# Weight sums of the output projection made in DRAM, and a rebuilt last stage, in a hybrid attention layer

## The chip, the cores and the metric

The kernel runs on one core of one Trainium2 chip. The metric is the device time of the program in microseconds (us), as the median of several runs. Before the change it is 952.56 us, the median of three runs from 950.74 to 953.96 us. One more execution was taken with the hardware profiler; all durations of single instructions come from that one.

## The reference, cut to what matters

One encoder layer in fp32 on 512 tokens of 2048 features, with 16 meta tokens put ahead of them (528 rows):

```
hn = rmsnorm(h, pre_norm_g)                       # h: (528, 2048)
qa, ka, va, ga, qb, kb, vb, gb = split(hn @ w_in)
ya = gqa_axial_mixer(qa, ka, va, ...) * silu(ga)  # mixer A: 8 heads of 128, 2 key/value heads, axial rope
yb = diff_attn_mixer(qb, kb, vb, ...) * silu(gb)  # mixer B: 8 heads, two softmaxes of 64 each, ALiBi
y  = concat([ya, yb]) @ w_out                     # (528, 2048) x (2048, 2048)
h  = h + rmsnorm(y, post_norm_g)                  # returned without the meta tokens
```

The change touches only the last two lines: the output projection, its RMSNorm and the residual sum. Mixer B is where part of the new work is put.

## The kernel before, in words

**Products and weights.** Every fp32 operand is split into a high part (rounded to fp32r) and a low part (the rest), and a product is three matmuls: high by high, low by high, high by low. `mm` (L63) issues them all. Weights come in chunks of 128x1024 (512 KB): `fetch` takes the next entry of the list `todo` two entries ahead of its use, `wload` puts the load on SP's queue (L151) into the tile `st` (three buffers), and `wsplit` makes `wh` on ACT (L158) and `wl` on DVE (L159), three buffers of each. An entry of `todo` that is a function is called in place of `wload`.

**Attention.** The program runs the input projection column by column as dense matmuls, and the attention of each head is laid between them by hand: generators in `lanes`, with delays in the table `LAG`. One head of mixer B takes about 56 us. Per head, DVE adds the ALiBi bias (L460), ACT takes the exponential (L468), DVE the reciprocal of the sum (L470), POOL multiplies by it (L473), DVE combines the two softmaxes (L475), PE transposes, ACT and DVE split the transposed result into `ph` (L313) and `pl` (L316), and PE multiplies by the values. POOL also has the small operations at L420. The output of a mixer B head is stored to DRAM as `oscr` and read back later.

**Output projection.** It has four column groups of 512. Groups 0 and 3 are made in full by `dense_out`, eight chunks each. Groups 1 and 2 are made as a 2 x 2 block product in Strassen's form as Winograd wrote it, with seven products for eight: the rows fall in two halves of 256 tokens (row tiles 0 and 1, and 2 and 3), the inner dimension in its two halves of eight heads. `block(r, c, i)` is chunk `i` of column group `1 + r` and inner half `c`; `C(r, x, u)` is that column group of row tile `2x + u`, kept in the tiles `y`. The products follow one another on PE, each with four weight chunks and 48 matmuls of 128x512; I name them by their operands in the code: y(0,0), y(1,0), t1, t2, y(1,1), t3, t4. The weights of the first two and of the last are plain blocks. Those of the others are sums: the first is block (1,0) + (1,1), for t1; block (0,0) is added for t2; block (0,1) is added for y(1,1); and the last is (0,0) + (1,0), for t3.

Before the change these sums are made in SBUF tiles `chain` (`ch` in the profile). During `dense_out(3)` POOL's queue loads block (1,0) plainly (L832) and adds (1,1) onto it by an adding transfer (L833). After each split of a chain tile, `summed` loads one further block into an `st` buffer on SP (L704) and DVE adds it (L705); for the last sum, (0,0) is loaded afresh (L701). The operands t1 to t4 are sums of half heads, loaded by `heads_of`, combined on DVE and split by `operand`; `fourth_sum`, with its two DVE additions from L842 on, runs beside t3.

**The end.** As a column group is done, ACT squares it with a sum (L855) into `ssy`, and the result is multiplied by the gain `gpB`: on DVE in `collect`, on POOL in `block_done` (L904). The row factor is made on POOL by an addition with a scale (L936) and a power of -0.5 (L938). `row_block` multiplies 512 columns by that factor and adds the residual rows on DVE (L947), or, as the variant `far`, on ACT and POOL (L944, L945), and stores them on SP. The residual rows are loaded by POOL's queue: four loads of 512 KB for tiles 0 and 1 (L955), eight of 256 KB for tiles 2 and 3 (L960), placed in the code behind t3. In t4 the first chunk is used for both row tiles, and the other three for tile 0 in full, then for tile 1; `end(u, ps)` follows each: a subtraction (L976), the square, the gain (L978), the row factor and the row blocks. A scheduler with priorities orders each engine's instructions; those called through `keep_in_program_order` keep the order of the code among themselves.

## Time and the profile before

| | |
|---|---|
| median of three runs | 952.56 us (950.74 to 953.96) |
| profiled execution, its own time | 948.18 us |
| its span | 946.3 us |
| mean granted clock of PE | 0.992 |
| PE busy | 923.7 us (98%) |
| DVE busy | 584.5 us (62%) |
| ACT busy | 487.5 us (52%) |
| POOL busy | 142.2 us (15%) |
| SP's and ACT's queue, q1 | 104.71 MB, 34.0% of 16 engines' span |
| POOL's queue, q0 | 11.54 MB, 4.1% |

PE is TensorE, DVE VectorE, ACT ScalarE, POOL GpSimd, and SP the engine that mostly issues transfers; SPq and POOLq are their queues. The chain of work that ended last, followed back from the last instruction, is 87% PE and 6% DVE. PE is busy nearly all the time; in the page's 40 slices of the span only the last shows it at 3 tenths. A row of a timeline has the start in us, the duration in us, the engine, the line, the operation, output and inputs with their shapes, and in square brackets how long the engine stood idle ahead of it and what ended that. A row of a group ends with busy time and mean ns of one. The times of the last products, by the first row of each in PE's timeline, are those in the prediction.

### The profile page before, as it was taken

What the parts mean: (1) busy time and instruction counts of PE and PEld (TensorE: products, weight loads), DVE (VectorE), ACT (ScalarE), POOL (GpSimd) and SP (SyncE); (2) the same over time, 40 slices, a digit from 0 to 9 for tenths busy, and PEclk for the clock granted to TensorE, in tenths of its full rate; (3) what the DMA queues carried; (4) which work ended last, traced back from release to release, by engine and by line L of the source; (5) the groups of instructions that cost most, each with busy time, mean ns of one, the idle gap of its engine ahead of it and who ended that gap; (6) DMA issues with size and microseconds to landing.
All of it is one profiled execution on the core that took longest, in us unless ns stands there. A gap on an engine that the chain in (4) does not pass through costs nothing.

```text
span 946.3 us, 14242 instructions
## 1 busy us (share of the span) xinstructions
PE 923.7 (98%) x5498; PEld 810.6 (86%) x5498; DVE 584.5 (62%) x1007; ACT 487.5 (52%) x845; POOL 142.2 (15%) x186
## 2 busy tenths in 40 slices
PE   9999999999999999999999999999999999999993
PEld 8899898989989899998998888888888888888872
DVE  6386575747566584866655255448554662576996
ACT  6664655637464463745643154445655743244541
POOL 0001010100001010000111041126111113300044
PEclk9999999999999999999999999999999999999996
DMA  9843222322223122222223223121222447966785
GB/s 338 257 162 99 68 88 68 101 77 92 85 68 112 67 98 79 79 84 73 79 71 97 89 77 105 65 78 57 86 71 78 131 141 204 303 219 192 222 284 205
DMA packets 40611, 117.16 MB, mean 124 GB/s; under 512 B 4672, under 2 KB 9536, under 8 KB 40416
## 3 DMA queue, kind: packets, MB, share of 16 engines
q1 hardware_dynamic: 37072, 104.71, 34.0%
q0 software_dynamic: 3328, 11.54, 4.1%
q8 instruction: 43, 0.70, 0.3%
q14 instruction: 24, 0.20, 0.1%
q10 hardware_dynamic: 144, 0.01, 0.0%
HBM read 107.85 MB, written 8.39 MB: 123 GB/s over the span
## 4 chain that ended last, share of the span: by engine, by line
PE 87%; DVE 6%; ACT 2%; POOL 2%; issue 2%; DMA 1%; DVEq 0%; POOLq 0%; ACTq 0%
PE pd L63 55%; PE po L63 16%; PE sc L63 6%; PE pv L63 5%; PE tr L66 5%; DVE wl L159 1%; DVE qn L583 1%; DVE y L947 1%; DMA st<-in_w_o_dram 1%; POOL qn L597 1%; DMA xns<-in_xn_dram 1%; PE hot L63 0%; ACT qn L655 0%; ACT jk L580 0%; PE ss L63 0%
## 5 line engine op out<-in xcount | busy, mean ns | idle before, releaser
L63 PE MATMUL pd<-xh,wh 128*128 128x264 f32 (+1 forms) x992 | 332.8, 335 | 0.0
L63 PE MATMUL pd<-xh,wl 128*128 128x264 f32 (+1 forms) x992 | 324.3, 327 | 0.3 <-DVE wl L159 0.3
L63 PE MATMUL pd<-xl,wh 128*128 128x264 f32 (+1 forms) x992 | 324.6, 327 | 0.0
L158 ACT ACTIVATE wh<-st 128x1024 fp32r<-128x1024 f32 (+2 forms) x135 | 139.9, 1039 | 190.2 <-issue 82.7
L159 DVE TENSOR_TENSOR wl<-st,wh 128x1024 fp32r<-128x1024 f32 (+2 forms) x135 | 162.2, 1202 | 108.3 <-ACT wh L158 106.7
L63 PEld LDWEIGHTS pd<-xh,wl 128*128 128x128 f32 x992 | 186.5, 188 | 17.5 <-DVE wl L159 0.7
L63 PEld LDWEIGHTS pd<-xh,wh 128*128 128x128 f32 x992 | 187.2, 189 | 12.6 <-ACT wh L158 0.2
L63 PEld LDWEIGHTS pd<-xl,wh 128*128 128x128 f32 x992 | 187.3, 189 | 11.1
L63 PE MATMUL po<-wh,oh 128*128 128x512 f32 x176 | 70.5, 401 | 0.0
L63 PE MATMUL po<-wh,ol 128*128 128x512 f32 x176 | 69.5, 395 | 0.9 <-DVE ol L316 0.9
L63 PE MATMUL po<-wl,oh 128*128 128x512 f32 x176 | 69.4, 394 | 0.0
L468 ACT ACTIVATE p<-p,mx 128x528 f32<-128x528 f32 x64 | 47.1, 736 | 43.0 <-DVE mx L460 42.7
L473 POOL TENSOR_SCALAR p<-p,sm 128x528 f32<-128x528 f32 x32 | 23.2, 725 | 268.2 <-DVE sm L470 251.5
L313 ACT ACTIVATE ph<-tr 128x512 fp32r<-128x512 f32 x64 | 37.7, 592 | 36.4 <-PE tr L66 36.1
L460 DVE CUSTOM_DVE_ANT_0 p<-sc,dist 128x528 f32<-128x528 f32 x64 | 44.9, 701 | 13.4 <-PE sc L63 13.0
L63 PE MATMUL pd<-wh,xh 128*128 128x512 f32 x128 | 52.0, 407 | 0.8 <-DVE vf L307 0.8
L316 DVE TENSOR_TENSOR pl<-tr,ph 128x512 fp32r<-128x512 f32 x64 | 43.3, 687 | 14.5 <-ACT ph L313 14.1
L66 PE MATMUL tr<-ident,p 128*128 128x128 f32 (+1 forms) x320 | 50.6, 272 | 1.4 <-DVE gA L563 1.4
L63 PE MATMUL pd<-wl,xh 128*128 128x512 f32 x128 | 50.4, 394 | 0.0
L63 PE MATMUL pd<-wh,xl 128*128 128x512 f32 x128 | 50.2, 392 | 0.0
L66 PEld LDWEIGHTS tr<-ident,p 128*128 128x128 f32 (+1 forms) x320 | 37.4, 131 | 12.6 <-DVE gA L563 1.9
L420 POOL TENSOR_SCALAR pm<-pm 32x256 fp32r<-32x256 f32 x32 | 20.0, 625 | 164.7 <-ACT pm L313 164.1
(206 smaller groups left out, 1554.3 us busy)
## 6 DMA issues: line engine op xcount, KB each, us to landing
st<-in_w_t_dram SPq DMA_DIRECT2D x82, 512.0 KB, 3.6
st<-in_w_o_dram SPq DMA_DIRECT2D x40, 512.0 KB, 4.2
st<-in_w_q_dram SPq DMA_DIRECT2D x16, 512.0 KB, 3.6
xs<-in_xT_dram SPq DMA_DIRECT2D x16, 264.0 KB, 5.2
xns<-in_xn_dram SPq DMA_DIRECT2D x8, 512.0 KB, 5.4
ch<-in_w_o_dram POOLq DMA_DIRECT2D x8, 512.0 KB, 7.9
out_dram<-y SPq DMA_DIRECT2D x16, 256.0 KB, 2.2
os<-oscr SPq DMA_DIRECT2D x6, 512.0 KB, 3.7
```

The source lines that it names most:

```text
L63: self._add(self.nc.tensor.matmul(out, lhsT, rhs, start=start, stop=stop), us)
L66: self._add(self.nc.tensor.transpose(out, in_, ident), 0.109)
L158: nc.scalar.activation(wh[:, c], st[:, c], AF.Copy)
L159: nc.vector.tensor_tensor(out=wl[:, c], in0=st[:, c], in1=wh[:, c].bitcast(F32), op=ALU.subtract)
L313: nc.scalar.activation(dst, src, AF.Copy)
L316: nc.vector.tensor_tensor(out=dst, in0=src, in1=h.bitcast(F32), op=ALU.subtract)
L420: nc.gpsimd.tensor_scalar(out=pm[32:64], in0=pm[0:32].bitcast(F32), scalar1=1.0, scalar2=1.0, op0=ALU.mult, op1=ALU.mult)
L460: nc.vector.tensor_tensor_reduce(out=two(p), in0=sc[:, :, :HALF], in1=two(dist[:, w0:w0 + NT]), scale=-0.125, scalar=3.0e38, op0=ALU.add, ...
L468: nc.scalar.activation(p2[m], p2[m], AF.Exp, scale=-1.0, bias=mx[:, m:m + 1], accum_out=sm[:, m:m + 1])
L473: nc.gpsimd.tensor_scalar(out=p2[0], in0=p2[0], scalar1=sm[:, 0:1], scalar2=1.0, op0=ALU.mult, op1=ALU.mult)
L583: nc.vector.scalar_tensor_tensor(out=raw[:, i, :], in0=raw[:, i, :], scalar=ss[:rows, i:i + 1], in1=g[:rows], op0=ALU.mult, op1=ALU.mult)
L597: nc.gpsimd.tensor_tensor(out=x, in0=x, in1=cos, op=ALU.mult)
```

## The change

It has two parts.

**Sums in DRAM.** The four sums live in 16 DRAM tiles `ws`, four for each sum (`sums[0]` to `sums[3]`, in the order above). `weigh` makes them one step at a time: it starts the adding transfer of the step before on POOL's queue (L708 of the new kernel) and the plain copy of the next step, from DRAM to DRAM, on SP's queue in program order. It is called three times in each of the heads 1 to 6 of mixer B and once in head 7, so 16 copies and 16 adds. The output projection then loads the sums as plain chunks; `chain`, its loads, its adding transfers and the twelve additions on DVE go. PE's order of matmuls stays as it is.

**The last stage.** The last product's block (1,1) is loaded into tiles `wx` while y(1,1) runs, and `apart` splits it as halves of 512 columns into slots of `oh` and `ol` that are free by then. `residual` loads one block of 128x512 of the residual rows on SP in each of the 16 steps of t1, t2, y(1,1) and t3, into other freed slots. C(0,1)'s interim sum is kept in C(1,1). POOL's gain multiplications move to DVE. The row factor becomes two small POOL operations ahead of time (`part`), a square root on ACT, whose table is loaded once early (`warm`), and a reciprocal on DVE. All row blocks are on DVE, and the end's order on DVE and ACT is fixed by `keep_in_program_order`.

The core of the diff:

```diff
-    def summed(add=None, fresh=None):
-        def step(i):
-            ws = wsplit(chain[i])
-            if fresh:
-                nc.sync.dma_start(out=chain[i], in_=block(*fresh, i))
-            if add:
-                st = wp.tile([P, 1024], F32, name="st", tag="st")
-                nc.sync.dma_start(out=st, in_=block(*add, i))
-                nc.vector.tensor_tensor(out=chain[i], in0=chain[i], in1=st, op=ALU.add)
...
+    steps = ([(sums[0][i], block(1, 0, i), block(1, 1, i)) for i in range(4)]
+             + [(sums[1][i], sums[0][i], block(0, 0, i)) for i in range(4)]
+             + [(sums[2][i], sums[1][i], block(0, 1, i)) for i in range(4)]
+             + [(sums[3][i], block(0, 0, i), block(1, 0, i)) for i in range(4)])
+    def weigh():
+        if adds:
+            dst, src = adds.pop(0)
+            nc.gpsimd.dma_start(out=dst, in_=src, accum_op=ALU.add)
+        if steps:
+            dst, src, add = steps.pop(0)
+            load(dst, src)
+            adds.append((dst, add))
+    def apart():
+        def step(i):
...
+            for j in range(2):
+                n = 8 + 2 * i + j
+                wh, wl = [op.tile([P, 512], F32R, name=f"w{x}", tag=f"o{x}{n}") for x in "hl"]
+                src = last[i][:, j * 512:(j + 1) * 512]
+                with tc.high_priority(rank[0]):
+                    hi(wh, src)
+                    lo(wl, src, wh)
...
-    todo += summed((1, 0), fresh=(0, 0)) + summed() + plain(1, 1)
+    for n in range(4):
+        todo += sums[n]
+    todo += apart()
...
+    def residual():
+        t, g = places[len(xres)]
+        n = len(xres)
+        x = op.tile([P, 512], F32, name="xr", tag=f"o{'hl'[n // 8]}{n % 8}")
+        load(x, xn[t * P:(t + 1) * P, g * 512:(g + 1) * 512])
...
-        TTp(out=C(r, x, u), in0=C(r, x, u), in1=gpB[:, g * 512:(g + 1) * 512], op=ALU.mult)
+        TTv(out=C(r, x, u), in0=C(r, x, u), in1=gpB[:, g * 512:(g + 1) * 512], op=ALU.mult)
...
+    for u, ps in enumerate(product(of_y(1, 1), pd, lambda i: load(last[i], block(1, 1, i)), late=True)):
...
-        nc.gpsimd.tensor_scalar(out=r, in0=ssy[t][:, 3:4], scalar1=sspart[t], scalar2=1.0 / DM,
-                                op0=ALU.add, op1=ALU.mult)
-        nc.gpsimd.tensor_tensor(out=r, in0=r, in1=mhalf[:, 0:1], op=ALU.pow)
+        order(nc.scalar.activation(r, r, AF.Sqrt, scale=1.0 / DM, bias=sspart[t]))
...
+    def turned(t):
+        order(nc.vector.reciprocal(out=ry[t], in_=ry[t]))
...
+    def end(u, ps):
+        last_block(u, ps)
+        by_gain(u)
+        if u == 0:
+            for g in (0, 3, 1, 2):
+                row_block(3, g)
+            turned(0)
+            for g in (0, 3):
+                row_block(0, g)
         else:
...
+            for g in (1, 2):
+                row_block(0, g)
+            turned(1)
+            for g in (0, 3, 1, 2):
+                row_block(1, g)
```

How the instructions move is shown at three places; the line numbers of added or later rows are those of the new kernel. First POOL in mixer B, in a head that has three adding transfers; `p` and `sm` are a softmax's exponentials and the reciprocal of their sum, `pm` a small operand of that head, `ws_549` to `ws_551` tiles of the second sum:

```order
-L473 TENSOR_SCALAR p<-p,sm 128x528 x3
-L420 TENSOR_SCALAR pm<-pm 32x256
+L708 DMA ws_550<-in_w_o_dram 128x1024
+L473 TENSOR_SCALAR p<-p,sm 128x528 x2
+L708 DMA ws_549<-in_w_o_dram 128x1024
 L473 TENSOR_SCALAR p<-p,sm 128x528
 L420 TENSOR_SCALAR pm<-pm 32x256
-L473 TENSOR_SCALAR p<-p,sm 128x528 x3
-L420 TENSOR_SCALAR pm<-pm 32x256
+L708 DMA ws_551<-in_w_o_dram 128x1024
```

The adding transfers stand between the softmax multiplications, which keep their own order.

Next SP around y(1,1), before. `st` and `ch` are as above:

```order
L704 DMA st<-in_w_o_dram 128x1024 x3
L701 DMA ch_8156<-in_w_o_dram 128x1024
L704 DMA st<-in_w_o_dram 128x1024
L701 DMA ch_8157<-in_w_o_dram 128x1024
L704 DMA st<-in_w_o_dram 128x1024
L701 DMA ch_8158<-in_w_o_dram 128x1024
L701 DMA ch_8159<-in_w_o_dram 128x1024
L151 DMA st<-in_w_o_dram 128x1024 x4
```

And there after the change; `xr` is a block of residual rows, `wx` a chunk of the last product's block, `ws_555` to `ws_558` are chunks of the third and fourth sum:

```order
L151 DMA st<-ws_555 128x1024
L143 DMA xr<-in_xn_dram 128x512
L143 DMA wx_8204<-in_w_o_dram 128x1024
L151 DMA st<-ws_556 128x1024
L143 DMA xr<-in_xn_dram 128x512
L143 DMA wx_8205<-in_w_o_dram 128x1024
L151 DMA st<-ws_557 128x1024
L143 DMA xr<-in_xn_dram 128x512
L143 DMA wx_8206<-in_w_o_dram 128x1024
L151 DMA st<-ws_558 128x1024
```

The loads for the sums are gone, and each step has a chunk of a sum, a block of rows and a chunk of the last product in their place.

Last DVE at the end, before. `y_8162` and `y_8163` are row tiles 0 and 1, `y_8164` and `y_8165` tiles 2 and 3; `po` is a product, `ry` a row factor, `xr` residual rows:

```order
L159 TENSOR_TENSOR wl<-st,wh 128x1024
L947 SCALAR_TENSOR_TENSOR y_8164<-y_8164,ry,xr 128x512 x3
L947 SCALAR_TENSOR_TENSOR y_8165<-y_8165,ry,xr 128x512
L976 TENSOR_TENSOR y_8162<-y_8162,po 128x512
L947 SCALAR_TENSOR_TENSOR y_8165<-y_8165,ry,xr 128x512 x2
L978 TENSOR_TENSOR y_8162<-y_8162,gpB 128x512
L947 SCALAR_TENSOR_TENSOR y_8162<-y_8162,ry,xr 128x512 x2
L976 TENSOR_TENSOR y_8163<-y_8163,po 128x512
L947 SCALAR_TENSOR_TENSOR y_8162<-y_8162,ry,xr 128x512
L947 SCALAR_TENSOR_TENSOR y_8165<-y_8165,ry,xr 128x512
L978 TENSOR_TENSOR y_8163<-y_8163,gpB 128x512
L947 SCALAR_TENSOR_TENSOR y_8163<-y_8163,ry,xr 128x512 x3
```

And after, from tile 0's subtraction on; `y_8210` to `y_8213` are row tiles 0 to 3, and the `ssy` tiles hold the row factors:

```order
L987 TENSOR_TENSOR y_8210<-y_8210,po 128x512
L993 TENSOR_TENSOR y_8210<-y_8210,gpB 128x512
L981 SCALAR_TENSOR_TENSOR y_8213<-y_8213,ssy_8217,xr 128x512 x4
L996 RECIPROCAL ssy_8214<-ssy_8214 128x1
L981 SCALAR_TENSOR_TENSOR y_8210<-y_8210,ssy_8214,xr 128x512 x2
L987 TENSOR_TENSOR y_8211<-y_8211,po 128x512
L993 TENSOR_TENSOR y_8211<-y_8211,gpB 128x512
L981 SCALAR_TENSOR_TENSOR y_8210<-y_8210,ssy_8214,xr 128x512 x2
L996 RECIPROCAL ssy_8215<-ssy_8215 128x1
L981 SCALAR_TENSOR_TENSOR y_8211<-y_8211,ssy_8215,xr 128x512 x4
```

Tile 1's subtraction now stands behind the four row blocks of tile 3 and two of tile 0, and its four row blocks are all on DVE.

More of the change, by code (lines that the diff above doesn't have):

```diff
@@ L679 @@
             todo += col(T_GA + h if h < NH else T_GB + h - NH)
-    chain = {}
+    last = {}
     def block(r, c, i):
@@ L735 @@
             v = values(pss)
+            if h:
+                weigh()
             ks = keys_B(dense_T(KEYS))
@@ L819 @@
     for i in range(4):
-        chain[i] = yp.tile([P, 1024], F32, name=f"ch{i}", tag=f"ch{i}")
+        last[i] = yp.tile([P, 1024], F32, name=f"wx{i}", tag=f"wx{i}")
     t1, t2, t3, t4 = [], [], [], []
@@ L829, in first_sums @@
         t2.append(operand("v", i, a1))
-    def first_chain(i):
-        nc.gpsimd.dma_start(out=chain[i], in_=block(1, 0, i))
-        nc.gpsimd.dma_start(out=chain[i], in_=block(1, 1, i), accum_op=ALU.add)
     def third_sum(i):
@@ L860, in collect, with product @@
         TTv(out=y[t][:, gs], in0=ps, in1=gpB[:, gs], op=ALU.mult)
-    def product(ops, pool, beside=None, done=None):
+    def product(ops, pool, beside=None, done=None, late=False):
         pss = [pool.tile([P, 512], F32, name="po", tag="pd") for _ in range(2)]
         def step(u, i, ws):
-            wh, wl = ws
             for j in range(2):
@@ L887, in product @@
         return pss
+    xres, places = {}, [(t, g) for t in (2, 3, 0, 1) for g in (0, 3, 1, 2)]
+    def residual():
[3 more added lines that the diff above has]
+        load(x, xn[t * P:(t + 1) * P, g * 512:(g + 1) * 512])
+        xres[t, g] = x
     def of_y(c, x):
@@ L920 @@
         block_done(0, 0, u)
-    for u, ps in enumerate(product(of_t(t1), pd2)):
+        part(u)
+    for u, ps in enumerate(product(of_t(t1), pd2, late=True)):
         nc.scalar.activation(C(1, 1, u), ps, AF.Copy)
-    for u, ps in enumerate(product(of_t(t2), pd2, third_sum)):
+    for u, ps in enumerate(product(of_t(t2), pd2, third_sum, late=True)):
         TTv(out=C(1, 0, u), in0=ps, in1=C(1, 0, u), op=SUB)
-        TTv(out=C(0, 1, u), in0=C(1, 0, u), in1=C(1, 1, u), op=ALU.add)
-    for u, ps in enumerate(product(of_y(1, 1), pd)):
-        TTv(out=C(0, 1, u), in0=ps, in1=C(0, 1, u), op=SUB)
+        TTv(out=C(1, 1, u), in0=C(1, 0, u), in1=C(1, 1, u), op=ALU.add)
@@ L939, in row_scale, with row_block @@
         return r
-    def row_block(t, r, x, g, far=False):
+    def row_block(t, g):
         v = y[t][:, g * 512:(g + 1) * 512]
-        if far:
-            nc.scalar.activation(v, v, AF.Copy, scale=r)
-            TTp(out=v, in0=v, in1=x, op=ALU.add)
-        else:
-            nc.vector.scalar_tensor_tensor(out=v, in0=v, scalar=r, in1=x, op0=ALU.mult,
-                                           op1=ALU.add)
-        load(out[t * P:(t + 1) * P, g * 512:(g + 1) * 512], v)
-    xl_ = [[yp.tile([P, 1024], F32, name="xr", tag=f"ch{2 * t + n}") for n in range(2)]
-           for t in range(2)]
@@ L966 @@
-    with tc.high_priority(AHEAD):
-        for t in range(2):
-            r = row_scale(2 + t)
-            for g in range(4):
-                row_block(2 + t, r, xh_[t][g], g)
-    xs = lambda t, g: xl_[t][g // 2][:, g % 2 * 512:(g % 2 + 1) * 512]
-    rs = []
-    def end(u, ps):
-        TTv(out=C(1, 0, u), in0=C(1, 0, u), in1=ps, op=SUB)
-        square(u, 2, C(1, 0, u))
-        TTv(out=C(1, 0, u), in0=C(1, 0, u), in1=gpB[:, 1024:1536], op=ALU.mult)
-        if u == 1:
-            row_block(0, rs[0], xs(0, 1), 1)
-            row_block(0, rs[0], xs(0, 2), 2)
-        rs.append(row_scale(u))
-        row_block(u, rs[u], xs(u, 0), 0, True)
-        for g in ((3,) if u == 0 else (3, 1, 2)):
-            row_block(u, rs[u], xs(u, g), g)
+        order(nc.vector.scalar_tensor_tensor(out=v, in0=v, scalar=ry[t], in1=xres[t, g],
+                                             op0=ALU.mult, op1=ALU.add))
@@ new lines, in row_block, with last_block, by_gain @@
+        load(out[t * P:(t + 1) * P, g * 512:(g + 1) * 512], v)
+    def last_block(t, ps):
+        v = y[t][:, 1024:1536]
+        order(TTv(out=v, in0=v, in1=ps, op=SUB))
+        order(square(t, 2, v))
+        ry[t] = row_scale(t)
+    def by_gain(t):
+        v = y[t][:, 1024:1536]
+        order(TTv(out=v, in0=v, in1=gpB[:, 1024:1536], op=ALU.mult))
+    def turned(t):
+        order(nc.vector.reciprocal(out=ry[t], in_=ry[t]))
+    ry = {}
+    pss = product(of_t(t3), pd, fourth_sum, late=True)
```

64 lines of the change are left out of this document (39 added, 25 removed).

## The prediction

> **What bounds the kernel now.** I read the page first, then the stretches, then PE's timeline of the last stage, the chain that ended last, and the timelines of DVE, ACT, POOL and SP at the places the change touches. The page's slices of the transfers, first to last:
> ```profile
> DMA  9843222322223122222223223121222447966785
> GB/s 338 257 162 99 68 88 68 101 77 92 85 68 112 67 98 79 79 84 73 79 71 97 89 77 105 65 78 57 86 71 78 131 141 204 303 219 192 222 284 205
> ```
> They are heavy only at both ends; 338 GB/s, with the queues nine tenths busy, is the most that any 23.7 us of this trace show. In the stretches view, the last 46 us:
> ```profile
> 900.00:946.30 46.30, 29.85 (x114) 22.56 (x112) 38.24 (x50) 13.92 (x23) 23.03 (x26) 0.84 0.70 243
> ```
> PE (second number) is busy for 29.85 of 46.30 us, at a mean granted clock of 0.84, while DVE (fourth) is busy for 38.24. PE's timeline there:
> ```profile
> 903.94 0.39 PE L63 MATMUL po<-wh,uh 128*128 128x512 f32 x1
> ...
> 915.78 0.39 PE L63 MATMUL po<-wh,vh 128*128 128x512 f32 x1
> ...
> 920.09 0.39 PE L63 MATMUL po<-wh,vl 128*128 128x512 f32 x1
> 921.59 0.50 PE L63 MATMUL po<-wl,vh 128*128 128x512 f32 x1 [1.12 <-DVE wl L159]
> ...
> 925.16 0.80 PE L63 MATMUL po<-wh,vh 128*128 128x512 f32 x1 [2.37 <-ACT wh L158]
> ...
> 933.62 0.39 PE L63 MATMUL po<-wl,vh 128*128 128x512 f32 x1
> ```
> The first row opens t3, the second t4, the last closes t4; each has 48 matmuls. Nineteen steps from 915.78 to 920.09 make 0.227 us from start to start. By that t3 would take 10.89 us and took 11.84 (0.95 lost), and t4's last matmul would start 10.66 us after its first and started 17.84 after it (7.18 lost). Of the 7.18, the five steps from 920.09 to 925.16 took 5.07 us for 1.13, so 3.94 went to the two marked gaps; the 23 steps behind took 8.46 us for 5.22, so 3.24 went to a lower clock after the second gap. What the gaps waited for stands in the chain that ended last:
> ```profile
> 908.78 3.40 DVE ts L842 x2
> ...
> 915.81 8.13 DMA st<-in_w_o_dram
> 924.05 1.07 ACT wh L158
> ```
> The last weight chunk was issued at 915.81, took 8.13 us to land among the row loads of POOL's queue, and was split only then; before it DVE stood in two ops that ran beside POOL's multiplication (3.40 for two). So this stage is bound by the work that readies weights, on DVE and in the queues, and then by the chain behind the last matmul, on DVE:
> ```profile
> 930.56 1.40 DVE L947 SCALAR_TENSOR_TENSOR y<-y,ry,xr 128x512 f32<-128x512 f32 x2
> ...
> 934.70 0.68 DVE L976 TENSOR_TENSOR y<-y,po 128x512 f32<-128x512 f32 x1
> ...
> 938.44 3.08 DVE L947 SCALAR_TENSOR_TENSOR y<-y,ry,xr 128x512 f32<-128x512 f32 x3 [0.72 <-POOL ry L938]
> ```
> PE's last result is there at 933.62 + 0.39 = 934.01; the last DVE op ends at 938.44 + 3.08 = 941.52, and 4.78 us of stores and closing follow to 946.30.
>
> **The change part by part.** *Sums.* From 850 us on, by groups, DVE does:
> ```profile
> L705 DVE TENSOR_TENSOR ch<-ch,st 128x1024 f32<-128x1024 f32 x12 | 15.1, 1261 | 0.9 <-DMA ch<-in_w_o_dram 0.9
> L947 DVE SCALAR_TENSOR_TENSOR y<-y,ry,xr 128x512 f32<-128x512 f32 x14 | 12.2, 920 | 2.3 <-POOL ry L938 2.3
> L159 DVE TENSOR_TENSOR wl<-st,wh 128x1024 fp32r<-128x1024 f32 x10 | 12.2, 1222 | 6.5 <-ACT wh L158 6.5
> ...
> L316 DVE TENSOR_TENSOR vl<-ts,vh 128x512 fp32r<-128x512 f32 x4 | 2.6, 682 | 0.0
> ```
> and POOL:
> ```profile
> L904 POOL TENSOR_TENSOR y<-y,gpB 128x512 f32<-128x512 f32 x6 | 11.0, 1834 | 51.6 <-issue 44.9 <-ACT jko L855 6.7
> ```
> The twelve adds (15.1 us) go, as do POOL's six multiplications, four of which become DVE ops of 0.68 (2.7 us) and two of which join the tail. The last product's weights are split as halves into slots of their own while y(1,1) and t3 run, so nothing is left to split in t4. Is DVE on time for t3? From y(1,1)'s start, 48 steps or 10.9 us ahead of t3's at 903.94, it has six whole splits at 1.14 from start to start (0.08 under their length, since ops overlap), eight halves and eight other 128x512 ops at 0.60, 6.8 + 4.8 + 4.8 = 16.4 us, and must be done by t3's fourth step at 903.9 + 8.2 = 912.1: 19.1 us. That fits, by 2.7. At its thinnest, the third chunk of t3, whose split stands behind two squares and two halves, I find it done 0.2 before its use. I take t3 and t4 without a wait: 0.95 and 7.18 come back, and t4 runs from 914.83 to 925.49, its result there at 925.88; PE gains 8.13.
>
> *The tail* gives some back. Its new order on DVE is fixed, and by the rows above an add or subtraction costs 0.60 behind another op (0.68 less 0.08), a row block 0.66 (1.40 for two, less 0.08). ACT's part between the subtraction and the gain:
> ```profile
> 930.73 0.63 ACT L855 ACTIVATE jko<-y 128x512 f32<-128x512 f32 x1 [5.01 <-DVE y L976]
> 931.27 0.19 ACT L855 ACTIVATION_READ_ACCUMULATOR jko<-y 128x1 f32 x1
> ```
> and from DVE's timeline in mixer B:
> ```profile
> 175.51 0.16 DVE L470 RECIPROCAL sm<-sm 128x2 f32<-128x2 f32 x1
> ```
> That is 0.73 (930.73 to 931.46) for the square, and I put 0.09 for each hand-over between the two; the DVE row is the nearest to the new reciprocal, 0.19 with its hand-over. After t3, DVE has five 0.60 ops, two reciprocals and four row blocks, 6.0 us, ending at 921.1. Tile 0's result is there after 30 matmuls of t4, at 914.83 + 29 x 0.227 + 0.39 = 921.8. From there: subtraction to 922.57, square to 923.4, gain to 924.1, four row blocks to 926.7, reciprocal 926.9, two row blocks 928.25. Only then comes tile 1's subtraction, 2.4 after PE gave its result; with the same steps it ends at 928.9, square 929.75, gain 930.45, two row blocks 931.8, reciprocal 932.0, four row blocks 934.7. That is 6.8 before 941.52. The square root (between the 0.19 and the 0.63 of the ACT rows) hides behind the gain and two row blocks, 1.9 us; were it in the open it would cost at most that 0.63. The last six stores come 0.66 apart, 262 KB each, 397 GB/s against the 338 seen: between 0 and 0.6 more at the end; I take 0.4, as 338 is a rate seen here. **Sum: -6.4 us.**
>
> *Mixer B* gets 16 copies on SP and 16 adding transfers on POOL, not in the trace. The nearest rows, of POOL, SP, DVE and PE in one head:
> ```profile
> 175.84 0.71 POOL L473 TENSOR_SCALAR p<-p,sm 128x528 f32<-128x528 f32 x1 [5.76 <-DVE sm L470]
> 180.34 0.71 POOL L473 TENSOR_SCALAR p<-p,sm 128x528 f32<-128x528 f32 x1 [3.79 <-DVE sm L470]
> ```
> ```profile
> 171.97 0.33 SPq L510 DMA_DIRECT2D oscr<-gB  x1
> ```
> ```profile
> 184.53 0.68 DVE L316 TENSOR_TENSOR pl<-tr,ph 128x512 fp32r<-128x512 f32 x1
> ```
> ```profile
> 191.41 0.28 PE L63 MATMUL pv<-pl,vh 128*128 128x256 f32 x1
> ```
> and of transfers of the same size, a plain load and the adding ones of before:
> ```profile
> st<-in_w_o_dram SPq DMA_DIRECT2D x40, 512.0 KB, 4.2
> ```
> ```profile
> L833 POOL DMA_DIRECT2D ch<-in_w_o_dram x4: 869/888/927, 793.7 to 812.5; - x4
> ...
> DMA to landing us min/median/max: 6.1/7.9/11.9
> ```
> POOL reaches an add at 176.55, behind its second softmax multiplication of a head. The copy that this add waits for stands on SP behind the store at 171.97, so it starts at about 172.3 and lands, at the 4.2 of a plain load of its 512 KB, at 176.5. The add's issue takes 0.89 and POOL is free at 177.4, 2.9 before its next op at 180.34. Behind a blocked POOL, DVE would wait, and behind DVE's wait stands the split at 184.53, read by PE at 191.41: 6.2 us of cover more. A copy of 11.9 us, the longest adding transfer, would still stay within both. So I take nothing, with 0 to +1 us, and no gain, since PE has no wait there to lose. On SP the copies stand between weight loads and wait for adds issued a head earlier. The Trainium skill, SBUF — State Buffer, section "A bandwidth-pool intuition that's wrong (but worth ruling out)", says that a POOL-issued transfer of about 620 ns alone takes about 3100 when DVE locks POOL out of the port its descriptors go through. The issues here took 869 to 927 ns, with DVE about half busy; by the page's figure the sum would not move, but the copy's cover below would shrink by 2.2 us.
>
> *Queues at the end.* POOL's twelve row loads become sixteen on SP, and the four chunks of the last product go ahead of t3's. In y(1,1) each step's rows on SP carry 524 + 262 + 524 KB. At 338 GB/s that is 3.9 us for a step of 2.8: four steps leave 4.4 us of backlog. A chunk is issued about 2.4 us after PE ends the step six before its own, and three buffers give it 8.2 - 2.4 = 5.8 us until its split can start and 3 us more until the split must; with 4.2 to land, 4.6 are to spare. Just enough, so nothing in the sum. The Trainium skill, Perfetto Trace Analysis, section "Roofline", has the 16 DMA engines at about 435 GB/s. By that a step is 3.0 us and the backlog under 1 us; no slice here shows more than 338.
>
> **The rivals.** *Late chunks in y(1,1) and t3:* at 303 GB/s, the next lower slice, a step's transfers take 4.3 us and the backlog is 6.1, so PE waits 1.5 us; with a gap as above, 3.2 us of low clock follow: 4.7 back, 950.9 us. It decides below about 332 GB/s. For it: the 8.13 us landing above. Against: half of the queue's load then came from POOL's burst at the same moment.
>
> *POOL blocked in mixer B, slower:* if a copy within DRAM lands later than 2.9 + 6.2 us past the 4.2, that is over 13.3, PE waits in each of six heads. At 15.5 it is 2.2 x 6 = 13 us: 959 us. Against: DMA stands at 2 to 3 tenths there. For: no row has a transfer with both ends in DRAM. By the skill's figure for descriptors the point would be 11.1, within the 11.9 seen, which is worth some chance.
>
> *A slower tail:* if the twelve row blocks behind tile 0 cost the 0.92 that they averaged before (12.2 us for 14 in DVE's groups), 12 x 0.26 = 3.1 come back: 949.3. Against: those long ones ran beside POOL's adds, which the change takes away.
>
> **How the numbers follow.** The profiled execution took 948.18 us, 4.4 under the median of the three runs; -6.4 on it makes 941.8, and on the median of 952.56 it makes 946.2. Chances: forecast 0.68 (943.5 to 948.5), late chunks 0.15, slower tail 0.09, POOL blocked 0.08. 0.3%, about what a measurement of this kernel can tell from no change, is 2.9 us. Under 949.7 falls the forecast, half of the slower tails and a quarter of the late chunks: 0.77; within 2.9 us falls most of the rest of these two, 0.14; above, POOL blocked and a little of the late ones, 0.09. The range reaches down by the spread of the three runs and a tail without the 0.4 to 943, and up over the late chunks to 951.5.
>
> **What would show it.** Right: PE's waits in t3 and t4 gone and its clock full to the end; DVE without a gap from tile 0's subtraction on, the last row block 8 to 9 us after PE's last matmul; POOL's adds in mixer B with spare time behind each. Wrong: a PE wait for a split in y(1,1) or t3; row blocks of 0.9; POOL's softmax multiplications shifted in mixer B with PE waits for transposes or for pl; or a store queue that lands over 1 us later behind the last DVE op.

## The result and the profile after

The changed kernel takes 942.38 us (median of four runs, 941.11 to 944.20), the kernel before 951.65 us beside it (950.71 to 953.96): ratio 0.990, interval 0.9874 to 0.9927, so 9.3 us faster. The forecast was 946.2 us, in a range from 943.0 to 951.5, so the direction was right and the size was not: the median lies 0.6 us below the range. The profiled execution took 941.67 us with a span of 939.9, almost what the forecast gave for it (941.8); that hit was luck, as will be seen.

The page's slices of the transfers, the same two lines as in the prediction:

```profile
DMA  9755533644546364222322223212212263755874
GB/s 339 257 166 151 149 118 108 164 127 146 156 117 169 108 166 126 78 89 71 98 68 86 96 69 120 68 58 68 90 61 74 76 192 110 278 184 164 301 274 179
```

Slices 4 to 16 carry the copies and adding transfers of mixer B, some 50 GB/s more than before. The stretch from 900 us on:

```profile
900.00:939.90 39.90, 28.03 (x123) 22.61 (x121) 31.12 (x49) 13.38 (x27) 3.29 (x4) 0.91 0.53 200
```

POOL (sixth number) is down from 23.03 to 3.29 us, DVE from 38.24 to 31.12, and the mean clock is 0.91 in place of 0.84. PE's timeline, with the first matmul of t1, t3 and t4 and the last of t4:

```profile
872.96 0.40 PE L63 MATMUL po<-wh,uh 128*128 128x512 f32 x1
...
905.95 0.39 PE L63 MATMUL po<-wh,uh 128*128 128x512 f32 x1
...
916.86 0.40 PE L63 MATMUL po<-wh,vh 128*128 128x512 f32 x1
...
927.63 0.40 PE L63 MATMUL po<-wl,vh 128*128 128x512 f32 x1
```

None of the rows between has a wait: t3 takes 10.91 us, t4's last matmul starts 10.77 behind its first. The end of DVE's timeline:

```profile
930.21 0.68 DVE L987 TENSOR_TENSOR y<-y,po 128x512 f32<-128x512 f32 x1
931.67 0.69 DVE L993 TENSOR_TENSOR y<-y,gpB 128x512 f32<-128x512 f32 x1 [0.79 <-ACT jko L878]
932.28 1.41 DVE L981 SCALAR_TENSOR_TENSOR y<-y,ssy,xr 128x512 f32<-128x512 f32 x2
933.61 0.16 DVE L996 RECIPROCAL ssy<-ssy 128x1 f32<-128x1 f32 x1
933.80 2.74 DVE L981 SCALAR_TENSOR_TENSOR y<-y,ssy,xr 128x512 f32<-128x512 f32 x4
```

The last row block ends at 936.54, 3.36 us ahead of the span's end (4.78 before).

**A measure of the last stage.** Executions of one kernel differ by up to 3.65 us in when t1 starts (below). So I compare from t1's first matmul to the end of the span, in three parts: to PE's last result, on to DVE's last op, on to the end. Each number is a difference of a few rows like those above, and each line of the table is one trace. For the kernel before, t1's first matmul is this row:

```profile
870.95 0.40 PE L63 MATMUL po<-wh,uh 128*128 128x512 f32 x1
```

| kernel | PE | DVE | end | sum | ratio to the kernel before (interval) |
|---|---|---|---|---|---|
| before, first trace | 63.06 | 7.51 | 4.78 | 75.35 | |
| before_again | 66.65 | 6.45 | 4.74 | 77.84 | 0.9999 (0.9985 to 1.0012) |
| before_split_first | 56.84 | 14.95 | 4.79 | 76.58 | 1.0009 (0.9992 to 1.0025) |
| before_gain_dve | 59.60 | 11.56 | 4.74 | 75.90 | 0.9993 (0.9982 to 1.0004) |
| before_rows_early | 56.46 | 12.67 | 5.03 | 74.16 | 0.9977 (0.9965 to 0.9989) |
| before_pool_free | 55.21 | 12.89 | 5.05 | 73.15 | 0.9959 (0.9945 to 0.9974) |
| sums_only | 62.47 | 6.45 | 5.21 | 74.13 | 0.9967 (0.9955 to 0.9978) |
| tail_only | 55.05 | 12.17 | 3.54 | 70.76 | 0.9951 (0.9933 to 0.9969) |
| after, first trace | 55.07 | 8.51 | 3.36 | 66.94 | 0.9900 (0.9874 to 0.9927) |
| after_again | 55.07 | 8.51 | 3.37 | 66.95 | 0.9898 (0.9881 to 0.9915) |
| after_third | 55.07 | 8.50 | 3.33 | 66.90 | 0.9902 (0.9883 to 0.9921) |
| after_gain_pool | 55.07 | 8.50 | 3.32 | 66.89 | 0.9899 (0.9878 to 0.9920) |
| after_far_first | 55.07 | 8.85 | 4.78 | 68.70 | 0.9924 (0.9904 to 0.9944) |
| after_far_last | 55.07 | 8.85 | 3.91 | 67.83 | 0.9911 (0.9892 to 0.9930) |
| fast_gain | 55.07 | 6.94 | 3.32 | 65.33 | 0.9874 (0.9850 to 0.9897) |
| fast_end | 55.08 | 4.83 | 6.42 | 66.33 | 0.9899 (0.9878 to 0.9919) |
| fast_order | 55.07 | 5.67 | 3.34 | 64.08 | 0.9882 (0.9862 to 0.9902) |
| fast_order_again | 55.07 | 5.68 | 3.37 | 64.12 | 0.9869 (0.9847 to 0.9892) |

### The profile page after: what moved, and what is told of

It is laid out like the page before. It is cut to its first block, busy times and chain, and to the rows that moved or that the text cites. A ratio compares the mean times of both kernels' runs of the same rounds, so it can differ in the third digit from the quotient of the medians.

```text
span 939.9 us, 14273 instructions
## 1 busy us (share of the span) xinstructions
PE 920.1 (98%) x5498; PEld 808.2 (86%) x5498; DVE 570.6 (61%) x1003; ACT 488.2 (52%) x853; POOL 129.5 (14%) x174
## 4 chain that ended last, share of the span: by engine, by line
PE 85%; DVE 6%; ACT 3%; issue 2%; DMA 2%; POOL 2%; SPq 0%; DVEq 0%; POOLq 0%; ACTq 0%
PE pd L63 55%; PE po L63 16%; PE sc L63 5%; PE tr L66 5%; PE pv L63 4%; DVE qn L583 1%; DVE wl L159 1%; DVE y L981 1%; POOL qn L597 1%; DMA os<-oscr 1%; DMA xns<-in_xn_dram 1%; ACT jk L580 1%; DMA xs<-in_xT_dram 0%; DVE qn L598 0%; ACT qn L655 0%
## 5 line engine op out<-in xcount | busy, mean ns | idle before, releaser
L158 ACT ACTIVATE wh<-st 128x1024 fp32r<-128x1024 f32 (+2 forms) x147 | 152.8, 1040 | 215.5 <-issue 82.8
L159 DVE TENSOR_TENSOR wl<-st,wh 128x1024 fp32r<-128x1024 f32 (+2 forms) x147 | 177.0, 1205 | 126.0 <-ACT wh L158 124.4
```

Of the source, the lines that this page charges most:

```text
L158: nc.scalar.activation(wh[:, c], st[:, c], AF.Copy)
L159: nc.vector.tensor_tensor(out=wl[:, c], in0=st[:, c], in1=wh[:, c].bitcast(F32), op=ALU.subtract)
```

## The experiments

**The two kernels once more.** Both unchanged.

> The kernel before, unchanged, for more traces and clocks of it. The forecast of -6.4 us met the profiled executions (948.18 to 941.67), while the medians moved by 9.3 us, so something costs the kernel before some 3 to 4 us in ordinary executions that its one profiled execution did not have. Theory: that is the stall at the last weight chunk in t4, whose length changes from run to run with what the queues carry then; the runs then spread by 2 us and more, their mean clock lies below the 0.992 of the profiled execution (low clock behind a gap), and a trace of a run near 952 has gaps of 6 to 9 us in t3 and t4, not 3.9. Rival: an offset of every execution that lies outside the stages (start, closing); then gaps of 4 us again, and the extra time ahead of 50 us or behind the last matmul.

> The changed kernel, unchanged, as a control on the same chip: 942.4 us, 9.3 below the kernel before, by both theories. Its trace shows whether the 2.0 us that PE had lost by the start of t1 (0.4 by 50 us, 0.5 in a wait at 664, 1.1 at 759 to 767) come again: if they are of the change, within 0.3 us at the same places; if they are chance, they move by over 0.5.

> The changed kernel as the control: 66.95 us from t1's first matmul to the end of the span for the third time, within 0.1, whatever its start; the kernel before had 75.35 and 77.84 in two traces.

Measured: 949.94 us for before_again (12 runs, 948.64 to 953.36), 940.22 for after_again beside 950.01 before, 941.46 for after_third beside 950.77. In four batches, of 11 to 23 runs each, the kernel before had medians of 950.01 to 950.77, so about 2 us of the 4.4 between the profiled execution and the median of 952.56 came with those first three runs. The mean clocks of the twelve runs (0.990 to 0.993) lie around the 0.992 of the first trace, and not below it as my theory had it; the longer stall did come. The second trace of before is of an execution of 952.51 us, and its PE row in t4 is this:

```profile
922.66 0.50 PE L63 MATMUL po<-wl,vh 128*128 128x512 f32 x1 [1.27 <-DVE wl L159]
...
931.38 0.79 PE L63 MATMUL po<-wl,vh 128*128 128x512 f32 x1 [7.07 <-DVE wl L159]
```

So the stall is 8.34 us here, where the first trace had 3.5. What made it is in POOL's timeline of this execution, and in DVE's behind it:

```profile
909.09 7.82 POOL L904 TENSOR_TENSOR y<-y,gpB 128x512 f32<-128x512 f32 x2 [0.59 <-ACT jko L855]
916.85 0.59 POOL L955 DMA_DIRECT2D xr<-in_xn_dram  x1
...
924.20 0.54 POOL L960 DMA_DIRECT2D xr<-in_xn_dram  x1 [3.00 <-DMA xr<-in_xn_dram]
...
926.24 1.28 POOL L904 TENSOR_TENSOR y<-y,gpB 128x512 f32<-128x512 f32 x1
927.49 0.26 POOL L936 TENSOR_SCALAR ry<-ssy,ssp 128x1 f32<-128x1 f32 x1
927.83 0.57 POOL L938 TENSOR_TENSOR ry<-ry,mhalf 128x1 f32<-128x1 f32 x1
```
```profile
909.89 1.28 DVE L842 TENSOR_TENSOR ts<-vh,ts 128x512 f32<-128x512 f32 x2
...
928.44 1.75 DVE L947 SCALAR_TENSOR_TENSOR y<-y,ry,xr 128x512 f32<-128x512 f32 x1 [5.23 <-POOL ry L938]
930.11 1.21 DVE L159 TENSOR_TENSOR wl<-st,wh 128x1024 fp32r<-128x1024 f32 x1
```

Two multiplications on POOL took 7.82 us, while DVE went at full rate for the first 4.5 of them (1.28 for two). The row loads stand behind them on POOL, the row factor behind the row loads, DVE's first row block waits 5.23 us for the factor, and the last weight split stands behind that row block in DVE's order. In the first trace the same two multiplications went otherwise:

```profile
907.90 3.74 POOL L904 TENSOR_TENSOR y<-y,gpB 128x512 f32<-128x512 f32 x2 [0.59 <-ACT jko L855]
...
921.25 1.44 POOL L904 TENSOR_TENSOR y<-y,gpB 128x512 f32<-128x512 f32 x1 [3.35 <-ACT jko L855]
...
923.46 0.57 POOL L938 TENSOR_TENSOR ry<-ry,mhalf 128x1 f32<-128x1 f32 x1
```
```profile
908.70 3.49 DVE L842 TENSOR_TENSOR ts<-vh,ts 128x512 f32<-128x512 f32 x2
...
924.06 0.75 DVE L947 SCALAR_TENSOR_TENSOR y<-y,ry,xr 128x512 f32<-128x512 f32 x1 [0.83 <-POOL ry L938]
```

There it was DVE that lost time (3.49 us for the two at 908.70). POOL had its row loads out early and stood idle ahead of 921.25, so in this trace the row loads did not hold the factor; it waited for ACT's square of a block that DVE reached late. In the three traces of the changed kernel, t1 starts at 872.96, 870.65 and 874.30 us, and the sum is 66.90 to 66.95: the differences lie ahead of t1. The 2.0 us by which t1 was late in the first trace were chance, as one of the two theories had it: 0.4 were lost by 50 us, the rest in waits at 664 and from 759 to 767 us, and after_again has no such waits.

**Half of the change each.** (Of each diff only the core is shown.) For sums_only, the kernel before gets `weigh` and the tiles in DRAM, and loses `chain`:

```diff
-    todo += whole(0) + whole(3) + plain(0, 0) + plain(0, 1) + summed((0, 0)) + summed((0, 1))
-    todo += summed((1, 0), fresh=(0, 0)) + summed() + plain(1, 1)
+    todo += whole(0) + whole(3) + plain(0, 0) + plain(0, 1)
+    for n in range(4):
+        todo += sums[n]
+    todo += plain(1, 1)
```

For tail_only, the changed kernel gets `chain`, `first_chain` and `summed` of before in place of `weigh`, and the last block goes into their tiles:

```diff
+    def take(i):
+        last[i] = yp.tile([P, 1024], F32, name=f"wx{i}", tag=f"ch{i}")
+        load(last[i], block(1, 1, i))
```

> The kernel before with its four sums made in DRAM as in the changed kernel, and its last stage left as it was (rows by POOL's queue, gains and row factors on POOL, last block split late, order of the end). If the twelve additions on DVE are what made the last splits late, the last chunk's load is issued earlier, t4 loses most of its gaps and the kernel gains 3 to 6 us of the 9. If the stall comes from the row loads of POOL's queue that collide with the last chunk's landing, the gap stays at 2 to 4 us and the gain is 0 to 2 us.

> The changed kernel with the sums made in SBUF as before (POOL's loads, DVE's twelve additions, SP's extra loads), and the last stage as in the changed kernel; the last product's block goes into the tiles of the sums once these have been split, so it is loaded two steps later than in the changed kernel. DVE had 2.7 us to spare over y(1,1) and t3 by the forecast's count, and eight additions of 1.26 us come on top: late by 7 us. If the DVE is what counts there, PE waits in t3 or t4 for splits and most of the gain is gone: 948 to 953 us. If the end's new order and the rows' early loads carry the gain, 943 to 946.

Measured: 947.01 us (3.0 less than the 950.01 beside it) and 945.53 (4.5 less); the whole change makes 9.8 there. The 2.3 us that the two halves leave are no more than their intervals allow (1.1 to 1.7 us each way), so that they appear only with both is not shown. In sums_only PE still waits in t4 for a split behind a row block:

```profile
925.41 0.80 PE L63 MATMUL po<-wl,vh 128*128 128x512 f32 x1 [3.55 <-DVE wl L159]
```

Neither theory holds whole there: the gap stayed, as the rival had it, and the gain was that of the first. In tail_only the splits are not 7 us late, as my count had it, and the time falls in the second of the two ranges that I gave: PE waits for nothing in t3 and t4 (55.05 us, as in the changed kernel), though twelve additions more are on DVE. They push DVE's end back, 12.17 us behind PE in place of 8.51:

```profile
938.02 2.74 DVE L980 SCALAR_TENSOR_TENSOR y<-y,ssy,xr 128x512 f32<-128x512 f32 x4
```

So with the new end, the sums in DRAM are worth 3.8 us of this stage (70.76 less 66.94; 5.3 by the medians), nearly all of it behind PE's last result.

**Is it PE's stall?** before_split_first takes only the wait from the last split; the calls are the same, in an order that `keep_in_program_order` fixes (the lines that make the swap; the others hold the rest of the order):

```diff
+            keep.append(1)
             last = [fetch(len(todo)) for _ in range(3)]
+            rows()
```

> The kernel before with one swap on DVE: the last weight split stands ahead of the first row block of tile 2, which waits for its row factor from POOL; the rest of DVE's tail keeps its order, and POOL, ACT and SP theirs. Theory: in ordinary executions POOL's gain multiplications and row loads run late, the row factor comes 3 to 5 us late, and the split behind it makes PE wait (7.07 us in the second trace of before). With the swap that wait goes to under 1.5 us, but the row blocks still wait for the same POOL, so only part shows at the end: 1 to 3 us faster than before. Rival: PE waits for the landing of the last chunk among the row loads; then the swap changes nothing, within 0.5 us.

Measured: 951.61 us beside 950.67. PE's wait of 7.07 us is gone (1.13 and 0.16 are left in t4), and its last result comes 56.84 us after t1's start in place of 66.65. But the row blocks wait all the same:

```profile
923.39 1.22 DVE L159 TENSOR_TENSOR wl<-st,wh 128x1024 fp32r<-128x1024 f32 x1
929.01 4.43 DVE L953 SCALAR_TENSOR_TENSOR y<-y,ry,xr 128x512 f32<-128x512 f32 x5 [4.39 <-DMA xr<-in_xn_dram]
```
```profile
928.40 0.57 POOL L944 TENSOR_TENSOR ry<-ry,mhalf 128x1 f32<-128x1 f32 x1
```

The view puts the wait down to a row load, which landed at 929.00; the factor was ready at 928.97, so this trace cannot tell the two apart. DVE's last op ends 71.79 us after t1's start, where before_again had 73.10 and the first trace 70.57. Both theories fall in part: the swap frees PE by 9.8 us against before_again, as the first had it, and the median does not move, as the rival had it, but not for the rival's reason. In this kernel PE's stall was beside the path or nearly so: in the first trace no row of DVE behind 924.06 waits for PE, in the second only one does, for 0.73 us. The path went over POOL.

**POOL's part, piece by piece,** each on top of before_split_first: gains to DVE (`TTp` to `TTv` in `block_done`), rows loaded on SP by the changed kernel's `residual`, and both.

> The kernel with the last split ahead (before_split_first) and the four gain multiplications of block_done moved from POOL to DVE. New theory: the end of the kernel before is set by POOL, where two gain multiplications beside DVE take 7.82 us, the row loads stand behind them, and the row factor of tile 2 comes at 929 us; PE's stall in t4 is only a by-product. Without the multiplications the row loads go out some 7 us earlier and the factor comes near 924: 2 to 4 us faster than the kernel before. Rival: DVE was as full as POOL was late, and four more ops of 0.6 us on it, with the last additions of the sums, eat the gain: within 1 us.

> The kernel with the last split ahead, and the residual rows loaded on SP during t1 to t3 into freed tiles, as in the changed kernel, in place of POOL's queue; gains stay on POOL. By the theory of POOL's chain the row factor no longer waits behind row loads (4.39 us of DVE's idle time ended by a row load in before_split_first), and comes near 925: 3 to 5 us faster than the kernel before. Rival: the slow multiplications alone hold the chain, or SP's queue makes the sums' loads late: under 1.5 us faster.

> Both at once: last split ahead, rows loaded early on SP, gains on DVE; sums still made in SBUF with twelve additions on DVE. Theory: POOL's chain is gone whole, and what is left between this and the changed kernel is the DVE time of the additions, the split halves and the order of the end: 4 to 6 us faster than the kernel before. Rival: if the sums in DRAM or the early split of the last block carry the gain, under 3.

Measured: 949.35, 947.85 and 946.34 us beside 950.21, so 0.9, 2.4 and 3.9 less, in the second and third beyond the interval. (All six multiplications of `block_done` move, not four as I wrote.) For the rows alone I had expected 3 to 5, too much: the factor still stands behind a slow multiplication (2.04 us). Both together came out just under the 4 to 6 expected. For the gains alone 2 to 4 was wrong. The row loads do go out earlier, but the factor then waits for DVE, whose short reductions stand behind the last split:

```profile
926.60 0.27 POOL L942 TENSOR_SCALAR ry<-ssy,ssp 128x1 f32<-128x1 f32 x1 [9.50 <-DVE ssp L970]
```

With both, PE waits for nothing (55.21), DVE's row blocks follow without long waits, and its five runs lie within 1.4 us (945.70 to 947.14), where 23 of the kernel before span 5.2. That is under half of the whole gain.

These six traces agree on what sets the end. The factor of tile 2 is ready 53.08 and 55.64 us after t1's start in the two traces of before, and 55.85, 55.62, 53.18 and 52.57 in the four kernels from before_split_first to before_pool_free. From there to DVE's last op it is 17.5 us in both traces of before, and 15.5 to 16.0 in the four, while PE's last result moves between 55.2 and 66.7. So DVE's end follows the factor, and not PE. The rows that end the factor in before_gain_dve, before_rows_early and before_pool_free:

```profile
926.95 0.57 POOL L944 TENSOR_TENSOR ry<-ry,mhalf 128x1 f32<-128x1 f32 x1
```
```profile
926.55 0.57 POOL L955 TENSOR_TENSOR ry<-ry,mhalf 128x1 f32<-128x1 f32 x1
```
```profile
922.75 0.57 POOL L955 TENSOR_TENSOR ry<-ry,mhalf 128x1 f32<-128x1 f32 x1
```

**Gains back to POOL in the changed kernel** (`TTv` to `TTp` in `block_done`, nothing else):

> The changed kernel with its four gain multiplications behind y(1,0) and y(1,1) on POOL again; nothing else moves. Theory of a shared port: DVE's ops beside them take up to 3.4 us for two, as in the trace of before, DVE has 0.2 us to spare at its thinnest place, so splits for t3 come late and PE waits 1 to 2 us with a low clock behind: 943 to 945 where the changed kernel has 940.2 on this chip, 1 to 4 us slower. Rival: four DVE ops of 0.6 us less make up for it, and POOL is far from the path now: within 1 us.

Measured: 941.91 us, ratio 0.9899, and the last stage is 66.89: the rival was right. The multiplications in its last stage take 1.47 and 2.25 us on POOL, and of the DVE operations beside them one group loses 0.5 us and one operation 1.1, yet DVE's end and PE's stay where they were. Moving them was worth nothing once the rows and the factors no longer stood behind them.

**The closing.** The kernel before made one row block of tile 1 on ACT and POOL, and stored it first. I put this back:

```diff
             turned(1)
-            for g in (0, 3, 1, 2):
+            v = y[1][:, :512]
+            order(nc.scalar.activation(v, v, AF.Copy, scale=ry[1]))
+            order(TTp(out=v, in0=v, in1=xres[1, 0], op=ALU.add))
+            load(out[P:2 * P, :512], v)
+            for g in (3, 1, 2):
                 row_block(1, g)
```

In after_far_last the `load` stands behind the loop.

> The changed kernel with the first row block of tile 1 as in the kernel before: scaled on ACT, added on POOL, and its store ahead of the other three of that tile on SP. Theory on the mis-sized closing (4.78 us in the kernel before, 3.36 in the changed one, 5.18 forecast): SP's last four stores wait in order for POOL's addition and then go out together. DVE has one row block less but three that run beside POOL (3.08 us in the kernel before), so it ends within 0.5 us of the changed kernel; the time from DVE's last op to the end of the span goes from 3.4 to 4.6 to 5.0, and the last stage takes 67.8 to 68.5 us from t1's first matmul in place of 66.95. Rival: the closing has another cause (16 stores at another rate, the row factor on POOL) and stays at 3.4.

> The same with that store behind the other three. If the order on SP is what costs, the closing is 3.4 to 3.9 us and the last stage 0.7 to 1.2 us shorter than with the store first; if POOL's addition itself is what costs, both are alike.

Measured: closings of 4.78 and 3.91 us, sums of 68.70 and 67.83 for 66.95, as expected but for 0.2 us in the first sum. The rows at the end of after_far_first:

```profile
931.24 3.08 DVE L981 SCALAR_TENSOR_TENSOR y<-y,ssy,xr 128x512 f32<-128x512 f32 x3
```
```profile
932.04 1.73 POOL L1028 TENSOR_TENSOR y<-y,xr 128x512 f32<-128x512 f32 x1 [23.62 <-ACT y L1027]
```

POOL ends at 933.77, and only then can the first of SP's last four stores go; DVE, with three row blocks for four, is no sooner ready, since they take 1.03 us each beside POOL and 0.69 without. So the variant cost 1.75 us in all: 0.35 in DVE's end and 1.4 in the closing, 0.87 of these by its place in SP's order. The medians (943.92 and 941.89, beside 941.46 for after_third) agree within their intervals.

**A better end.** fast_gain writes the gain's result to a tile of its own, so that it need not wait for ACT's square of the same block, and takes tile 1's subtraction ahead of tile 0's row blocks. fast_end also has ACT scale tile 3's rows, which adding transfers then put onto output rows filled beforehand with the residual. fast_order has the gain's own tile for all four row tiles, with tile 2's and half of tile 3's row blocks ahead of tile 0's subtraction (the core; the lines that it takes out of `end` are left out):

```diff
-        order(TTv(out=v, in0=v, in1=gpB[:, 1024:1536], op=ALU.mult))
+        z[t] = yp.tile([P, 1024], F32, name="z", tag=f"wx{t}")[:, :512]
+        order(TTv(out=z[t], in0=y[t][:, 1024:1536], in1=gpB[:, 1024:1536], op=ALU.mult))
...
     def end(u, ps):
         last_block(u, ps)
         by_gain(u)
+        for g in (1, 2):
+            row_block(3 if u == 0 else 0, g)
+        turned(u)
+        for g in ((0, 3) if u == 0 else (0, 3, 1, 2)):
+            row_block(u, g)
```

> The changed kernel with two edits of its tail: the gain of the last column block goes to a tile of its own, so that DVE need not wait for ACT's square of the same block (0.79 us of idle time each for tiles 0 and 1), and tile 1's subtraction comes straight behind tile 3's row blocks, ahead of tile 0's. DVE is busy from tile 0's subtraction to the end then: 0.79 twice less, 1.5 to 1.9 us faster than the changed kernel. If the tail is set by stores or the closing and not by DVE: under 0.5.

> The same with tile 3's four row blocks off DVE: the output rows of tile 3 are filled with the residual rows by a copy in DRAM in mixer B, ACT multiplies by the row factor, and adding transfers on POOL's queue add the result. DVE saves 4 x 0.66 = 2.65 us behind tile 0's subtraction, and then waits for tile 1's result, 4.1 us behind tile 0's, with one row block, a gain, a reciprocal and four row blocks to do: 3.3 to 3.8 us faster than the changed kernel if DVE is the bound of the tail. Rival: the adding transfers (issue 0.84 to 1.1 us each, landing in 6 to 8 us) end last, some 4 us behind DVE's last op: under 1.5 us faster.

> The changed kernel with the gain of the last column block in tiles of its own for all four row tiles, and an order of the end without idle time on DVE: gain straight behind subtraction, all of tile 2's and half of tile 3's row blocks ahead of tile 0's subtraction, half of tile 0's ahead of tile 1's. By the rows of the changed kernel DVE's last op then ends 5.4 us behind PE's last result in place of 8.5: 2.8 to 3.2 us faster than the changed kernel, 12.5 us below the kernel before. If the stores are the bound by then (387 GB/s for 262 KB each is 0.68 us, as long as a row block): some 0.5 less.

> The kernel with the reordered end once more, beside the changed kernel on one chip: its last stage takes 64.1 us by its trace where the changed kernel has 66.95, so 2.5 to 3.2 us faster; if executions differ by chance ahead of the last stage by more than that, the medians may show 1.5 to 4.

Measured: fast_gain 939.21 us beside 950.67, last stage 1.6 us shorter, as expected. fast_order 938.55 beside 950.21, and 937.93 beside 941.46 for after_third: 3.5 us faster by the medians, 2.8 by the last stage. Its end:

```profile
928.52 2.07 DVE L981 SCALAR_TENSOR_TENSOR y<-y,ssy,xr 128x512 f32<-128x512 f32 x3
930.52 0.74 DVE L981 SCALAR_TENSOR_TENSOR z<-z,ssy,xr 128x512 f32<-128x512 f32 x1
```

This is 5.67 us behind PE's last result. fast_end is no faster than the changed kernel (941.89 beside 950.67, ratio 0.9899). DVE ends 4.83 us behind PE, the soonest of all and 2.1 sooner than in fast_gain, but the closing takes 6.42, 3.1 longer than there, as the rival had it. The landings from 915 us on, of plain stores and of adding ones:

```profile
out_dram<-y SPq DMA_DIRECT2D x10, 256.0 KB, 5.4
out_dram<-y POOLq DMA_DIRECT2D x4, 256.0 KB, 7.3
```

In the changed kernel, from 915 us on:

```profile
out_dram<-y SPq DMA_DIRECT2D x16, 256.0 KB, 2.1
```

## Why the prediction was right, and where it was wrong

Against the forecast's own steps, counted from t1's first matmul at 870.95:

- *PE's last result* was forecast at 925.88, 54.93 us after it; 55.07 was measured, three times. No wait in t3 or t4: right.
- *DVE's last row block* was forecast at 934.7, 63.75 after it; measured 63.58 (936.54 less 872.96). Right in mechanism and size, with the row block at 0.66 to 0.69; the rival of 0.92 fell, though 1.03 came back as soon as POOL added beside it.
- *The closing* was forecast at 4.78 + 0.4 = 5.18 us and took 3.36. This is the step of the sum that failed: a term of the wrong size. I took the 4.78 of before as a fixed cost of stores and made it longer, since the row blocks come closer together. But 1.4 us of it came with the block that POOL adds, 0.87 of that by its place ahead of SP's last stores, and the change removes it: with that block put back, the closing is 4.78 again. I had counted that block's time on DVE and did not ask which queue waited for POOL; after_far_first and after_far_last show it.

Together the stage was forecast at 68.95 and took 66.94. The profiled time still came out as forecast, because t1 started 2.0 us later in this execution by chance. That hid the 2.0 us that the stage was shorter than forecast, 1.8 of them in the closing.

- *From one execution to the median.* "-6.4 ... on the median of 952.56 it makes 946.2" took the profiled execution's stall for a usual one. The last stage of before took 75.35 us there and 77.84 in the second trace. Against the measured 66.94 that is a gain of 8.4 and of 10.9; the medians, 9.3 to 9.8, lie between. The profiled execution lay 4.4 us under the median of the three runs, and I had quoted this gap without asking what it was made of. So the 3.8 us between 946.2 and 942.4 are 2.0 of the stage, 0.9 by which the medians gained more than the first profiled stage (9.3 against 8.4), and 0.9 because the kernel before took 951.65 beside the result, not 952.56. With the closing alone put right, the forecast would have been 944.3.
- *What bounded the kernel.* "So this stage is bound by the work that readies weights, on DVE and in the queues" failed as a cause where it names the queues. The landing of the last chunk (8.13 us) let ACT split it at 924.05 in that one execution, with POOL's factor for tile 2 at the same moment (DVE's row block at 924.06 waited for it). In the second trace the chunk was there by 922.13 and the factor only at 928.40. before_split_first settles it: with PE nearly free of the stall, the stage took 76.58 us, between the 75.35 and 77.84 of the two traces of before. That DVE's crowded order made the factor late in the first trace fits its rows; no run isolates it. The forecast of the end was nevertheless close, since its tail was worked out anew and the change takes POOL's whole chain away: no row loads, no power and no far addition there.
- *The sums.* The count of DVE's work in y(1,1) and t3 was made to see whether PE would wait. tail_only shows that PE would not have waited with all twelve additions kept, though they are more than the 2.7 us to spare that I counted; what they cost is 3.7 us behind PE's last result.
- *Mixer B at nothing* was right. Between 50.2 and 663.9 us PE's instructions run in both traces at a distance of about 0.4 us, within 0.1 in all but one row, with all adds in between:

```profile
L708 POOL DMA_DIRECT2D ws<-in_w_o_dram x16: 842/844/1093, 77.0 to 358.6; - x16
...
  POOL ws L708: 83.7, 15
DMA to landing us min/median/max: 3.3/5.2/8.2
```

POOL stood 83.7 us in front of adds, up to 13 in one piece, and PE lost nothing by it; nothing landed later than 8.2 us where 13.3 would have been needed. The issues took 842 to 1093 ns. The Trainium skill (SBUF — State Buffer, section "A bandwidth-pool intuition that's wrong (but worth ruling out)") has about 3100 ns for a POOL-issued transfer beside a `tensor_copy` on DVE; that was not seen here.

- *Queues at the end:* no wait, so right in its result, and wrong in its rate. From 890 to 920 us the trace shows, in 40 slices of 0.75 us:

```profile
GB/s 210 311 350 279 227 317 380 418 407 429 385 431 404 434 396 410 404 391 415 434 380 404 404 393 384 246 45 0 0 0 0 22 0 0 0 0 0 0 0 0
...
st<-ws SPq DMA_DIRECT2D x5, 512.0 KB, 6.6
wx<-in_w_o_dram SPq DMA_DIRECT2D x4, 512.0 KB, 7.3
```

From 894.5 to 909 us it is 380 to 434 GB/s, not 338, which was a mean over 23.7 us and no limit: in slices of 0.5 us the trace of before has up to 402 GB/s as well. The landings were longer than the 4.2 that I took, 6.6 to 7.3 us, and the three buffers covered that. The figure of the Trainium skill (Perfetto Trace Analysis, section "Roofline", about 435) was the better one here.

How much each part of the change carries depends on the order in which one counts. From the second trace of before: POOL's chain with the row loads 4.7 us (before_pool_free, stall included; 3.9 by the medians, 2.2 from the first trace), the far variant and its store some 1.7, the twelve additions 3.7 to 3.8, and what is left to the new order. How often an ordinary execution of before has the long or the short multiplication on POOL stays open: two traces with the long one (one of them of before_split_first) and one with the short are too few.

## What to carry to other kernels

A stall on the busiest engine is worth what ends behind it: ask of the last operation, not of PE, what it waited for, and follow that through the orders of every engine on the way, here from DVE's row block over POOL's factor to its row loads and multiplications. Where the profiled execution lies off the median, take a second trace before pricing its waits, since a wait need not be the same in two executions of one program (3.5 and 8.34 us here). And the time behind the last compute operation is a term like any other: see which store came last, and what stood ahead of it in its queue.

## What the runs showed of the hardware

- Two 128x512 multiplications on POOL beside DVE took 3.74 us in one execution and 7.82 in another, while two additions on DVE at the same place took 3.49 and 1.28. The Trainium skill, SBUF — State Buffer, section "Who interferes with whom", says that a DVE operation with two SBUF inputs contends with a GpSimd one that reads SBUF, and that the order of issue decides who blocks. These rows agree with that; no run here isolates it. The two executions are of one program, and their last stages differ by 2.5 us.
- With four adding transfers of 256 KB to DRAM in flight in fast_end, plain stores of the same size landed in 5.4 us (median) in place of 2.1, and the closing lost more (3.1 us) than DVE had gained over fast_gain (2.1). No run has the adding transfers without the rest of that kernel's order.
- From t1 on, the changed kernel repeats to 0.05 us in three traces, while the start of t1 moves by 3.65 us between them. For a change in a late stage that repeats so well, a difference of two rows of the trace is sharper than a median of five runs.
